# Full stacks in groups D, C and B, one bank pool in the MLP, and B's second wave on VectorE

## The chip, the cores and the metric

The kernel runs on one core of a Trainium2 chip. The metric is the device time of one launch in microseconds (us). The core has five engines that run their own instruction lists in order: TensorE (PE in the profile; its weight loads are PEld), VectorE (DVE), ScalarE (ACT), GpSimd (POOL) and SyncE (SP, which here only issues DMAs). Semaphores order the engines against each other.

## The reference

A trunk of two layers over a sequence of 1024 tokens and a width of 1024, in float32. Each layer normalises, projects once into the inputs of four groups of heads, and adds an output projection and a squared-ReLU MLP to the residual:

```python
for l in range(DEPTH):                       # DEPTH = 2, x is 1024 x 1024
    h = rms_norm(x, norm1_g[l])
    (a_cq, a_ckv, a_kr, b_q, b_k, b_v, c_q, c_k, c_v,
     d_q, d_k, d_v) = split(h @ w_in[l])
    y_a = mla_mixer(a_cq, a_ckv, a_kr, ...)   # latent attention, 4 heads
    y_b = diff_mixer(b_q, b_k, b_v, ...)      # 4 heads, two softmaxes each, 32 wide
    y_c = swa_mixer(c_q, c_k, c_v, ...)       # window of +-128, 4 q and 2 kv heads
    y_d = na_mixer(d_q, d_k, d_v, ...)        # neighbourhood on a 64-wide grid
    x = x + concat(norm(y_a), y_b, norm(y_c), norm(y_d)) @ w_out[l]
    h = rms_norm(x, norm2_g[l])
    x = x + square(relu(h @ w_up[l])) @ w_down[l]   # hidden width 4096
return rms_norm(x, final_norm_g)
```

In group B each of four heads has two pairs of a 32-wide q and k; its output is the first softmax less a factor times the second, times V. q and k are rotated first (rope).

## The kernel before

**Numbers in two parts.** Each float32 operand is split into a rounded high part and a low part, the rest (`split`, line 191): ScalarE rounds (L195), and VectorE or GpSimd subtracts (L189). A product of two such operands is three matmuls: high by high (L221), high by low (L222), low by high (L223). So one tile of output, 128 x 512, over a width of 1024 takes 8 x 3 = 24 matmuls. Weights come by DMA into `ws` (two buffers), are rounded into `wh` and split into `wl` by GpSimd (`weights`; `wtile` makes the two halves of a weight tile that 48 matmuls use, 24 for each half of the tokens). Each `load` is a request of SyncE.

**The opening of a layer.** In the first wave (`several`) six banks gather Q, K and V of B's first part (t = 0). Each is then evicted: `ev_rope` for Q and K (VectorE multiplies with the tables and writes a temporary `part`, three buffers; a second `part` holds the swapped halves, and an addition gives the rotated sum), then `emit_parts` splits it into `both`, high and low, whose DMAs store it in DRAM as `qb`, `kb`. V is put on the token axis by transposes (`to_values`) and stored as `vb`. Two of the three eviction steps of `ev_rope` and the splits go to the engine that `self.eng` names. The second wave projects Q, K and V of the second part (t = 1) into banks `mm`, `sb`, `mm`, with `self.eng` set to GpSimd. Then `weave` interleaves B's attention with the projections of groups A and D, which serve as filler. The PSUM banks of this part are mm=2, tr=2, sb=3, pv=1.

**Stacks.** q and k come back from DRAM as a stack (`self.stack()`): 128 partitions whose rows are high and low parts one under the other, so that one matmul of the scores (L851) sums the products of the parts. In B a stack of q holds high, high, low and that of k high, low, high, 32 rows each, 96 rows, by three loads each. D and C fill 128 rows with halves of 64, by two loads a stack.

**Order in this part.** A scheduler places every instruction by a simulated timeline and by priorities (`high_priority`), so the order on an engine is not that of the code.

**The MLP.** TensorE's order is written out by hand there. Up and down projections each run as seven block products in place of eight, over sums and differences of blocks. The up half works through groups with banks q=4, u=2, p=2; block products p1 to p7 go to them, and the results, squared and rectified, are stored to DRAM as `acts`, operands 1 to 7 of the down half among them. The last group ends with p7 (bank `u`), a copy of it to `u3` (L1290), p4 (bank `u`) and p3 (bank `p`). The down half opens another pool, u=4 and p=4, and loops over j = 0 to 3; in each j it multiplies the weight blocks `a11`, `a12`, `a21`, `a22` and their sums (four each, `raw` tiles by DMA, high and low as `wh` and `wl`) with operands loaded from `acts` (`act`, rounded into `far`). A block is 12 matmuls: four slices of its weights times three passes. The operands come in the order 1, 2, 6, 7, 4, 5, 3. `settled` is the sum behind which some of this may be issued; `finish_up` holds the last work of the up half, called from within the down half.

## Time and profile before

| | |
|---|---|
| median of 3 runs | 2625.5 us (2624.66 to 2625.53) |
| the profiled execution | 2624.3 us, its span 2622.5 us |
| granted TensorE clock, mean | 0.983 |
| DMA | 385 MB, 147 GB/s over the span |
| PE, share of the chain that ended last | 67% |

The profiled execution is the device time of one launch; its span runs from its first to its last instruction. In the rows of a timeline stand the start in us, the duration in us, the engine, the line, the operation, output and inputs, the shape, and in brackets how long the engine had been idle before and what released it. Rows whose first column is a stretch such as `70.00:80.00` are windows: the length, then busy time (and number of instructions) of PE, PEld, DVE, ACT, POOL, then the mean granted clock, the mean busy share of the DMA engines, and GB/s.

### The profile page before, as it was taken

What the parts mean: (1) busy time and instruction counts of PE and PEld (TensorE: products, weight loads), DVE (VectorE), ACT (ScalarE), POOL (GpSimd) and SP (SyncE); (2) the same over time, 40 slices, a digit from 0 to 9 for tenths busy, and PEclk for the clock granted to TensorE, in tenths of its full rate; (3) what the DMA queues carried; (4) which work ended last, traced back from release to release, by engine and by line L of the source; (5) the groups of instructions that cost most, each with busy time, mean ns of one, the idle gap of its engine ahead of it and who ended that gap; (6) DMA issues with size and microseconds to landing.
All of it is one profiled execution on the core that took longest, in us unless ns stands there. A gap on an engine that the chain in (4) does not pass through costs nothing.

```text
span 2622.5 us, 37463 instructions
## 1 busy us (share of the span) xinstructions
PE 2512.9 (96%) x12320; PEld 2087.0 (80%) x12320; DVE 1922.8 (73%) x3403; ACT 1427.7 (54%) x2588; POOL 1120.9 (43%) x800
## 2 busy tenths in 40 slices
PE   8999988999999999999999999899999999999998
PEld 7778877787788887888887888777887888878887
DVE  7577768784986668887576767677849866678886
ACT  4577767673644444444426777676736444444445
POOL 2565643201045554554434656332011555545554
PEclk9999999999999999999999899999999999999999
DMA  5634498332154456444245445962221544655431
GB/s 171 196 102 130 132 276 262 91 89 61 53 169 157 153 186 232 158 149 141 96 126 161 110 132 153 314 196 84 73 73 48 189 145 158 236 194 166 130 116 65
DMA packets 191539, 385.00 MB, mean 147 GB/s; under 512 B 23712, under 2 KB 34928, under 8 KB 191344
## 3 DMA queue, kind: packets, MB, share of 16 engines
q1 hardware_dynamic: 176976, 356.90, 44.1%
q10 hardware_dynamic: 14368, 25.70, 2.8%
q8 instruction: 98, 1.61, 0.3%
q14 instruction: 97, 0.79, 0.1%
HBM read 261.20 MB, written 121.32 MB: 146 GB/s over the span
## 4 chain that ended last, share of the span: by engine, by line
PE 67%; DVE 8%; issue 5%; ACT 4%; DMA 3%; POOL 1%; SPq 0%; DVEq 0%; POOLq 0%; ACTq 0%
PE u L223 9%; PE u L221 9%; PE u L222 9%; PE p L223 5%; PE p L222 5%; PE p L221 5%; PE mm L221 4%; PE mm L222 4%; PE mm L223 4%; PE sb L851 2%; DVE p L853 2%; PE tr L887 2%; ACT p L856 2%; DVE ptl L189 1%; DVE part L189 1%
## 5 line engine op out<-in xcount | busy, mean ns | idle before, releaser
L189 POOL TENSOR_TENSOR wl<-raw,wh 128x512 fp32r<-128x512 f32 x424 | 603.8, 1426 | 695.0 <-ACT wh L195 679.1
L195 ACT ACTIVATE wh<-raw 128x512 fp32r<-128x512 f32 x448 | 281.0, 629 | 545.9 <-PE u L222 297.8
L189 POOL TENSOR_TENSOR wl<-ws,wh 128x512 fp32r<-128x512 f32 (+1 forms) x120 | 150.1, 1253 | 413.1 <-ACT wh L195 386.5
L223 PE MATMUL u<-far,wl 128*128 128x512 f32 x768 | 301.5, 393 | 6.5 <-POOL wl L189 6.5
L221 PE MATMUL u<-far,wh 128*128 128x512 f32 x768 | 301.1, 392 | 4.9 <-ACT wh L195 2.7
L222 PE MATMUL u<-far,wh 128*128 128x512 f32 x768 | 300.8, 392 | 0.0
L189 DVE TENSOR_TENSOR ptl<-tr,pth 128x512 fp32r<-128x512 f32 (+2 forms) x384 | 237.5, 628 | 74.8 <-ACT pth L195 73.6
L189 DVE TENSOR_TENSOR raw<-raw 128x512 f32<-128x512 f32 x256 | 229.2, 904 | 84.7 <-DMA raw<-in_w_up 42.7
L856 ACT ACTIVATE p<-p,nm 128x1024 f32<-128x1024 f32 x192 | 220.2, 1147 | 83.3 <-DVE nm L853 82.5
L195 ACT ACTIVATE pth<-tr 128x512 fp32r<-128x512 f32 (+2 forms) x384 | 206.1, 547 | 94.4 <-PE tr L887 61.0
L223 PE MATMUL p<-far,wl 128*128 128x512 f32 (+1 forms) x648 | 251.0, 387 | 3.0 <-DVE wl L189 3.0
L221 PE MATMUL p<-far,wh 128*128 128x512 f32 (+1 forms) x648 | 250.9, 387 | 0.0
L222 PE MATMUL p<-far,wh 128*128 128x512 f32 (+1 forms) x648 | 250.6, 387 | 0.0
L851 PE MATMUL sb<-stack 96*128 96x512 f32 x640 | 218.6, 422 | 14.2 <-DVE part L189 8.9
L189 DVE TENSOR_TENSOR far<-act,far 128x512 fp32r<-128x512 f32 x224 | 199.4, 925 | 13.2 <-ACT far L195 13.2
L189 POOL TENSOR_TENSOR p<-p 128x1024 f32<-128x1024 f32 x64 | 154.0, 2409 | 109.2 <-ACT p L939 107.5
L221 PE MATMUL mm<-xh,wh 128*128 128x512 f32 x480 | 191.0, 398 | 4.6 <-DVE part L189 4.6
L223 PE MATMUL mm<-xh,wl 128*128 128x512 f32 x480 | 190.1, 396 | 0.0
L222 PE MATMUL mm<-xl,wh 128*128 128x512 f32 x480 | 189.2, 394 | 0.0
L223 PEld LDWEIGHTS u<-far,wl 128*128 128x128 f32 x768 | 145.3, 189 | 38.1 <-POOL wl L189 7.9
L221 PEld LDWEIGHTS u<-far,wh 128*128 128x128 f32 x768 | 145.4, 189 | 36.7 <-ACT wh L195 3.6
L222 PEld LDWEIGHTS u<-far,wh 128*128 128x128 f32 x768 | 145.2, 189 | 31.3 <-DVE far L189 0.8
(256 smaller groups left out, 5958.5 us busy)
## 6 DMA issues: line engine op xcount, KB each, us to landing
act<-acts SPq DMA_DIRECT2D x224, 256.0 KB
raw<-in_w_up SPq DMA_DIRECT2D x128, 256.0 KB
acts<-ev SPq DMA_DIRECT2D x128, 256.0 KB
raw<-in_w_down SPq DMA_DIRECT2D x128, 256.0 KB
acts<-ev ACTq DMA_DIRECT2D x96, 256.0 KB
ws<-in_w_in SPq DMA_DIRECT2D x76, 256.0 KB
rz<-drows SPq DMA_DIRECT2D x40, 256.0 KB
stack<-kd SPq DMA_DIRECT2D x32, 256.0 KB
```

The lines of the kernel that those rows point to most:

```text
L189: return (eng or self.nc.vector).tensor_tensor(out=out, in0=a, in1=b, op=op)
L195: self.rounded = nc.scalar.activation(hi, src, AF.Copy)
L221: mm(ps, w[0], x[0][:, sl], start=start, stop=False)
L222: mm(ps, w[0], x[1][:, sl], start=False, stop=False)
L223: mm(ps, w[1], x[0][:, sl], start=False, stop=stop)
L851: self.nc.tensor.matmul(ps, q[:, qt * P:(qt + 1) * P], k[:, sl], start=i == 0, stop=i == len(passes) - 1)
L853: self.nc.vector.tensor_tensor_reduce(out=p[:, sl], in0=ps, in1=self.zero[:, 0:1].bitcast(F).broadcast_to([P, 512]), scale=-scale, scalar= ...
L856: self.nc.scalar.activation(p, p, AF.Exp, bias=nm[:, 1:2], scale=-1.0, accum_out=z)
L887: nc.tensor.transpose(t[:, k * 256 + i * P:k * 256 + (i + 1) * P], p[:, (j * 2 + k) * P:(j * 2 + k + 1) * P], self.ident)
```

## The change

1. **Stacks.** `qb` is laid out in DRAM with the two parts of each row next to each other, so a stack of B's q is one load of 128 rows (high and low alternating); a stack of k is two loads, the high parts into the even and the low parts into the odd positions, each row twice (`twice`). The scores then run over 128 rows, with all four products of the parts where they had three. A stack of D or C is one load. On SyncE's queue a run has 1237 requests where it had 1333; those for B's stacks go from 96 to 48 a run.
2. **First wave.** V's two banks are now both `tr`, K's `sb` and `pv`, and V is evicted ahead of Q and K. V's transposes of the second part use `tr` too.
3. **Second wave.** `self.eng` is VectorE there. The weights of K and V (four `ws` loads a layer) are asked for by ScalarE. The call of `catch_up` between product and eviction is left out. Over the run, GpSimd has 16 instructions fewer and VectorE 16 more.
4. **MLP.** One pool of banks, q=4, u=2, p=2, spans both halves. The down half's four accumulators `u[]` take `q` banks, its other blocks alternate between `u` and `p`. p4 and p3 of the last group are called after the first down block (m = 0); the third sum is made ahead of them and `settled` is set there. The split of operand 1 is not bound to `settled`. Operand 4 is loaded from within the loop over operand 7, behind `summed` and the last rounding.

```diff
+def twice(t):
+    return t.unsqueeze(1).broadcast_to([t.shape[0], 2, *t.shape[1:]])
...
-        self.load(st, src)
+        (queue or self.nc.sync).dma_start(st, src)
...
-        qb, kb, vb = dr([2, 2, 4, 16, 2, S], "qb"), dr([2, 2, 4, 16, 2, S], "kb"), dr([4, P, 8, P], "vb")
+        qb, kb, vb = dr([2, 4, 16, 2, 2, S], "qb").rearrange("t g f h a s -> a t g f h s"), dr([2, 2, 4, 16, 2, S], "kb"), dr([4, P, 8, P], "vb")
...
-                    self.ev_plain(rb, self.to_values(vb[2 * t:2 * t + 2], "tr" if t else "mm"))]
+                    self.ev_plain(rb, self.to_values(vb[2 * t:2 * t + 2], "tr"))]
...
-                        return [(self.bank(a), self.bank(b)) for a, b in (("sb", "sb"), ("sb", "tr"), ("tr", "pv"))]
+                        return [(self.bank(a), self.bank(b)) for a, b in (("sb", "sb"), ("sb", "pv"), ("tr", "tr"))]
...
-                    for ev, b in zip(evacs_b(0), banks):
+                    q, k, v = zip(evacs_b(0), banks)
+                    for ev, b in (v, q, k):
                         for n in range(2):
                             ev(n, b[n])
-                    self.eng = nc.gpsimd
-                    for t, ev, tag in zip(self.WAVES[1], evacs_b(1), ("mm", "sb", "mm")):
-                        ws = self.wtile(w_in(t))
+                    self.eng = nc.vector
+                    for i, (t, ev, tag) in enumerate(zip(self.WAVES[1], evacs_b(1), ("mm", "sb", "mm"))):
+                        ws = self.wtile(w_in(t), nc.scalar if i else None)
                         for n in range(2):
                             ps = self.bank(tag)
                             self.product(ps, ws, xs, n)
-                            self.catch_up()
                             ev(n, ps)
+                    self.eng = nc.gpsimd
...
-                for i, (a, b) in enumerate(((0, 0), (0, 1), (1, 0))):
-                    self.load(qf[i * 32:(i + 1) * 32], run(qb[a, t, g]))
-                    self.load(kf[i * 32:(i + 1) * 32], run(kb[b, t, g]))
-                qk.append([(q[0:96], k[0:96])])
+                self.load(qf, twice(qb[:, t, g].rearrange("a f h s -> (f h a) s")))
+                for i in range(2):
+                    self.load(kf[i::2], twice(run(kb[i, t, g])))
+                qk.append([(q, k)])
...
-            self.mlp_up(l, acts)
-            self.mlp_down(l, acts)
+            with self.banks(q=4, u=2, p=2):
+                self.mlp_up(l, acts)
+                self.mlp_down(l, acts)
...
+            def third(s):
+                s.sum = self.tt(s.u3, s.p, s.u3, ALU.add)
...
-            p4(s)
-            p3(s)
+            third(s)
             self.settled = s.sum
+            def products():
+                p4(s)
+                p3(s)
...
-            self.finish_up = [free, rest]
+            self.finish_up = [products, free, rest]
...
-                u = [self.bank("u") for _ in M]
+                u = [self.bank("q") for _ in M]
...
+                b = [self.rows_split(self.far(), v) for v in t]
                 with ExitStack() as behind:
                     if j == 0:
                         behind.enter_context(tc.issue_after(self.settled.ins))
-                    b = [self.rows_split(self.far(), v) for v in t]
                     for m in M:
                         self.block(u[m], a11[m], b)
+                        if m == 0 and j == 0:
+                            self.finish_up.pop(0)()
...
-                        ps = self.bank("p")
+                        ps = self.bank("up"[m % 2])
...
-                with behind(passed):
-                    b = op(4)
+                    if m == 1:
+                        with behind(summed), behind(self.rounded):
+                            c = op(4)
+                b = c
...
-                p = [self.bank("p") for _ in M]
+                p = [self.bank("up"[m % 2]) for m in M]
```

What the order of the instructions becomes at three places follows. In a row stand the line, the operation, output and inputs, and the shape; a name's number tells instances apart, and differs between the two kernels.

The first place is GpSimd's order in the opening of layer 0, during the second wave: `wl` are its weight splits (`ws_571` and `ws_577` hold the weights of K, 655 and 661 those of V, 809 those of the first projection behind B), `part` and `both` the additions and splits of the evictions (524 and 530, 560 and 566 of Q's two halves, 608 and 614 of K's first). Before:

```order
L189 TENSOR_TENSOR wl_574<-ws_571,wh_573 128x512
L189 TENSOR_TENSOR wl_580<-ws_577,wh_579 128x512
L189 TENSOR_TENSOR part_524<-part_524,part_525 128x512
L189 TENSOR_TENSOR both_530<-part_524,both_530 128x512
L189 TENSOR_TENSOR wl_658<-ws_655,wh_657 128x512
L189 TENSOR_TENSOR wl_664<-ws_661,wh_663 128x512
L189 TENSOR_TENSOR part_560<-part_560,part_561 128x512
L189 TENSOR_TENSOR both_566<-part_560,both_566 128x512
L189 TENSOR_TENSOR wl_812<-ws_809,wh_811 128x512
L189 TENSOR_TENSOR part_608<-part_608,part_609 128x512
L189 TENSOR_TENSOR both_614<-part_608,both_614 128x512
```

After, from the same split on:

```order
L194 TENSOR_TENSOR wl_574<-ws_571,wh_573 128x512
L194 TENSOR_TENSOR wl_580<-ws_577,wh_579 128x512
L194 TENSOR_TENSOR wl_658<-ws_655,wh_657 128x512
L194 TENSOR_TENSOR wl_664<-ws_661,wh_663 128x512
L194 TENSOR_TENSOR wl_806<-ws_803,wh_805 128x512
L194 TENSOR_TENSOR wl_812<-ws_809,wh_811 128x512
L194 TENSOR_TENSOR wl_985<-ws_982,wh_984 128x512
```

Weight splits now follow one another; the additions and splits of the evictions have left this engine.

The second place is ScalarE's order in the same opening: `wh` are roundings of weights, `both<-part` those of the evictions of Q and K, `both<-mm` or `both<-tr` those of V, and DMA rows its requests (before, `wh_471` and `wh_477` are Q's weights; `both_427` and `both_438` are Q, 449 and 460 K). Before:

```order
L195 ACTIVATE wh_471<-ws_469 128x512
L195 ACTIVATE wh_477<-ws_475 128x512
L195 ACTIVATE both_427<-part_421 128x512
L195 ACTIVATE wh_573<-ws_571 128x512
L195 ACTIVATE both_438<-part_432 128x512
L195 ACTIVATE both_449<-part_443 128x512
L195 ACTIVATE both_460<-part_454 128x512
L195 ACTIVATE wh_579<-ws_577 128x512
L681 ACTIVATE both_511<-mm_506 128x8x64
L195 ACTIVATE wh_657<-ws_655 128x512
```

After:

```order
L200 ACTIVATE wh_489<-ws_487 128x512
L200 ACTIVATE wh_495<-ws_493 128x512
L212 DMA ws_571<-in_w_in 128x512
L212 DMA ws_577<-in_w_in 128x512
L200 ACTIVATE wh_573<-ws_571 128x512
L212 DMA ws_655<-in_w_in 128x512
L687 ACTIVATE both_428<-tr_423 128x8x64
L687 ACTIVATE both_439<-tr_434 128x8x64
L200 ACTIVATE wh_579<-ws_577 128x512
L200 ACTIVATE both_449<-part_443 128x512
L212 DMA ws_661<-in_w_in 128x512
L200 ACTIVATE wh_657<-ws_655 128x512
```

The roundings of V have moved ahead, the weight requests stand among the roundings, and `wh_579` and `wh_657` stand before the roundings of Q's two halves (`both_449`, and `both_460` behind the rows shown). On TensorE, the first score of B had 96 products and four transposes of the second wave ahead of it in the order; it has 20 + 28 + 48 + 44 = 140 products, with V's eight transposes after the first 20. Stretches of B's scores and value products with no projection product among them, longer than 24 instructions, were one in each layer (99 instructions with 17 scores in layer 0, 90 with 16 in layer 1) and are three (24, 53 and 95 instructions with 3, 11 and 14 scores in layer 0; 24, 59 and 41 with 3, 11 and 8 in layer 1).

The third place is ScalarE's order at the seam between the MLP's halves in layer 0. Of the weight roundings `wh`, those of `raw_10107` to `raw_10113` are the four blocks `a11`, those of `raw_10234` and `raw_10238` the first two of `a21`; `far<-act` are the roundings of operand 5. Before:

```order
L195 ACTIVATE wh_10358<-raw_10107 128x512
L195 ACTIVATE wh_10375<-raw_10109 128x512
L195 ACTIVATE far_10614<-act_10606 128x512
L195 ACTIVATE far_10617<-act_10608 128x512
L195 ACTIVATE wh_10392<-raw_10111 128x512
L195 ACTIVATE far_10620<-act_10610 128x512
L195 ACTIVATE wh_10409<-raw_10113 128x512
L195 ACTIVATE far_10623<-act_10612 128x512
L195 ACTIVATE wh_10446<-raw_10234 128x512
L195 ACTIVATE wh_10464<-raw_10238 128x512
```

After, where `raw_10027` to `raw_10033` are `a11`, `raw_10186` to `raw_10198` are `a21`:

```order
L200 ACTIVATE wh_10310<-raw_10027 128x512
L200 ACTIVATE wh_10327<-raw_10029 128x512
L200 ACTIVATE wh_10344<-raw_10031 128x512
L200 ACTIVATE wh_10361<-raw_10033 128x512
L200 ACTIVATE wh_10398<-raw_10186 128x512
L200 ACTIVATE wh_10416<-raw_10190 128x512
...
L200 ACTIVATE far_10658<-act_10650 128x512
L200 ACTIVATE far_10661<-act_10652 128x512
L200 ACTIVATE wh_10454<-raw_10194 128x512
L200 ACTIVATE wh_10472<-raw_10198 128x512
```

The four roundings of `a11` and two of `a21` stand together; behind them come ten activations (four of operand 4, four of operand 5 and the two shown of operand 3), then the other two of `a21`. TensorE's order at the seam was p7, p4, p3, then the down half's four blocks `a11`; it is p7, the block m = 0, p4, p3, the blocks m = 1 to 3, then the `a12` blocks alternating between banks `u` and `p`.

More of the change, by code (lines that the diff above doesn't have):

```diff
@@ L200, in split, with weights @@
                 out=lo, in0=src, scalar=scale, in1=hi.bitcast(F), op0=ALU.mult, op1=ALU.subtract)
-    def weights(self, src, pool=None, tag="w", bufs=3, keep=None):
+    def weights(self, src, pool=None, tag="w", bufs=3, keep=None, queue=None):
         pool = pool or self.wp
@@ L212, in weights, with wtile @@
         return [(wh[:, k], wl[:, k]) for k in range(n)]
-    def wtile(self, src):
-        return self.weights(src[0]) + self.weights(src[1])
+    def wtile(self, src, queue=None):
+        return self.weights(src[0], queue=queue) + self.weights(src[1], queue=queue)
     def passes(self, ps, w, x, sl, start, stop, **more):
@@ L1083, in attn_d @@
                 rows = slice(h2 * 64, (h2 + 1) * 64)
-                for i in range(2):
-                    half = slice(i * 64, (i + 1) * 64)
-                    self.load(qs.bitcast(F)[half], qd[i, t, rows])
-                    self.load(ks[0].bitcast(F)[half], kd[0, t, rows])
-                for i in range(2):
-                    self.load(ks[1].bitcast(F)[i * 64:(i + 1) * 64], kd[1, t, rows])
+                self.load(qs.bitcast(F), qd[:, t, rows].rearrange("i r s -> r i s"))
+                for i, k in enumerate(ks):
+                    self.load(k.bitcast(F), twice(kd[i, t, rows]))
                 v = self.vtile(vd[h])
@@ L1113, in attn_c @@
             for n, k in enumerate(ks):
-                for i in range(2):
-                    self.load(k.bitcast(F)[i * 64:(i + 1) * 64], run(kc[n, kv]))
+                self.load(k.bitcast(F), twice(run(kc[n, kv])))
             v = self.vtile(vc[kv])
@@ L1120, in attn_c @@
                 qs = self.stack()
-                for i in range(2):
-                    self.load(qs.bitcast(F)[i * 64:(i + 1) * 64], run(qc[i, kv, g]))
+                self.load(qs.bitcast(F), qc[:, kv, g].rearrange("a f h s -> (f h) a s"))
                 z, es, nm = (self.col(n, 8) for n in ("z0", "z1", "nb8"))
@@ L1228, in mlp_up @@
         sub = lambda o, a, b: self.tt(o, a, b, ALU.subtract)
-        with self.banks(q=4, u=2, p=2):
+        with ExitStack():
             near = lambda tag: [(self.piece(tag, R, "oph"), self.piece(tag, R, "opl")) for _ in range(4)]
@@ L1290, in p7 @@
                 nc.scalar.activation(s.u3, s.u, AF.Copy)
+            def third(s):
+                s.sum = self.tt(s.u3, s.p, s.u3, ALU.add)
             def p4(s):
-                s.sum = self.tt(s.u3, s.p, s.u3, ALU.add)
+                if s.sum is None:
+                    third(s)
                 self.block(s.u, s.c["22"], ops[4], start=False)
@@ L1320, in group @@
             def group(q):
-                s = SimpleNamespace(q=q, c=weights(q))
+                s = SimpleNamespace(q=q, c=weights(q), sum=None)
                 return s
@@ L1432, in mlp_up @@
                 held = s
-            p4(s)
-            p3(s)
+            third(s)
             self.settled = s.sum
+            def products():
+                p4(s)
+                p3(s)
             def free():
@@ L1458, in mlp_down @@
         sub = lambda o, a, b: self.tt(o, a, b, ALU.subtract)
-        with self.banks(u=4, p=4):
+        with ExitStack():
             def add(m, n, ps):
@@ L1516, in mlp_down @@
                     self.block(u[m], a11[m], b, start=False)
-                    add(m, 1, u[m])
+                    summed = add(m, 1, u[m])
                 with behind(passed):
@@ L1602, in final @@
             yield
-        ps = self.bank("u", [P, w // P])
+        ps = self.bank("q", [P, w // P])
         self.col_sums(ps, acc, self.ones[:, 0:1], range(w // P))
@@ L1609, in final @@
         yield
-        rb = self.bank("u")[:, :w]
+        rb = self.bank("q")[:, :w]
         for t in range(w // P):
```

## The prediction

> **What bounds the kernel now.** I read the page's head and chain first, then the timeline of TensorE with its idle times, and for each idle time the timelines of the engines behind it.
>
> ```profile
> span 2622.5 us, 37463 instructions
> PE 2512.9 (96%) x12320; PEld 2087.0 (80%) x12320; DVE 1922.8 (73%) x3403; ACT 1427.7 (54%) x2588; POOL 1120.9 (43%) x800
> PE 67%; DVE 8%; issue 5%; ACT 4%; DMA 3%; POOL 1%; SPq 0%; DVEq 0%; POOLq 0%; ACTq 0%
> ```
>
> TensorE is busy for 96% of the span and holds two thirds of the chain. The change alters none of its products in number or width, so the time can only move by TensorE's waits, and by matmuls that run at half pace after a wait. The undisturbed pace is 23.00/102 = 0.226 us for a 512-column matmul; the next stretch below it runs at half the granted clock, 13 matmuls in 5.60 us.
>
> ```profile
> 1037.00:1060.00 23.00, 23.00 (x102) 19.00 (x101) 13.21 (x17) 9.68 (x16) 10.77 (x9) 1.00 0.64 211
> 1031.40:1037.00 5.60, 5.60 (x13) 4.42 (x14) 4.96 (x7) 3.04 (x5) 3.47 (x3) 0.50 0.87 301
> ```
>
> I price a wait by start times: from the last matmul before it to the first at the old pace, less the nominal time of what ran between.
>
> **The opening of the attention: what it costs.** These are TensorE's rows around its waits, first layer 0, then layer 1.
>
> ```profile
> 57.23 0.39 PE L223 MATMUL sb<-xh,wl 128*128 128x512 f32 x1
> 58.95 0.66 PE L677 MATMUL mm<-ident,part 128*128 128x128 f32 x4 [1.34 <-DVE part L189]
> 60.39 0.39 PE L222 MATMUL sb<-xl,wh 128*128 128x512 f32 x1
> 61.29 0.50 PE L223 MATMUL sb<-xh,wl 128*128 128x512 f32 x1 [0.52 <-POOL wl L189]
> 83.53 0.39 PE L851 MATMUL sb<-stack 96*128 96x512 f32 x1
> 87.76 0.50 PE L851 MATMUL sb<-stack 96*128 96x512 f32 x1 [3.84 <-DVE part L189]
> 91.69 0.39 PE L222 MATMUL mm<-xl,wh 128*128 128x512 f32 x1
> ...
> 1355.41 0.39 PE L223 MATMUL sb<-xh,wl 128*128 128x512 f32 x1
> 1357.14 0.66 PE L677 MATMUL mm<-ident,part 128*128 128x128 f32 x4 [1.34 <-DVE part L189]
> 1358.58 0.40 PE L222 MATMUL sb<-xl,wh 128*128 128x512 f32 x1
> 1359.48 0.51 PE L223 MATMUL sb<-xh,wl 128*128 128x512 f32 x1 [0.50 <-POOL wl L189]
> 1381.73 0.39 PE L851 MATMUL sb<-stack 96*128 96x512 f32 x1
> 1387.15 1.53 PE L851 MATMUL sb<-stack 96*128 96x512 f32 x2 [5.03 <-DVE part L189]
> 1392.28 0.40 PE L222 MATMUL mm<-xl,wh 128*128 128x512 f32 x1
> ```
>
> The transposes of V cost 1.72 - 0.23 = 1.49 and 1.50 us, the late `wl` 0.67 and 0.67. The first scores cost more: between 83.53 and 91.69 stand three scores, four transposes and four products, nominally some 2.0 us, so 6.2 us are lost; in layer 1, 10.55 us less 2.65 (three more products) is 7.9. Together **18.4 us**: 4.3 small, 14.1 at the first scores. Who held the first scores is read one engine back at a time:
>
> ```profile
> 86.31 1.39 DVE L189 TENSOR_TENSOR part<-sb,tabs 64x512 f32<-64x512 f32 x2 [5.72 <-POOL part L189]
> 83.80 1.26 POOL L189 TENSOR_TENSOR wl<-ws,wh 128x512 fp32r<-128x512 f32 x1 [6.37 <-ACT wh L195]
> 85.02 1.26 POOL L189 TENSOR_TENSOR part<-part 128x512 f32<-128x512 f32 x1
> 83.09 0.63 ACT L195 ACTIVATE wh<-ws 128x512 fp32r<-128x512 f32 x1 [7.03 <-DMA ws<-in_w_in]
> 79.23 0.36 SPq L160 DMA_DIRECT2D ws<-in_w_in  x1
> ```
>
> The score needs its `sb` bank, which VectorE empties for B's K of the second wave. VectorE waits for GpSimd's add, because that add frees a `part` buffer. GpSimd is in order and its add stands behind a weight split that waits for weights, which SyncE asked for only among the stack loads.
>
> **What the change does there.** GpSimd's eight second-wave operations per layer go to VectorE, so its order holds weight splits alone and no `part` buffer hangs on a weight transfer. V of the first wave is evicted first; its transposes now stand behind 20 products (4.5 us) instead of waiting. In the new order the first score stands behind 20+28+48+44 = 140 products and eight transposes of the second wave, where it was behind 96 and four; this gives the stacks time. Added work: 16 VectorE operations in all, against a row like the second below some 0.65 us each, 10.4 us, laid where VectorE stood idle for up to 5.72 us. If that cover failed, the bank of the second wave's V would be late.
>
> Is anything late next? The second wave starts at 46.58.
>
> ```profile
> 46.58 0.39 PE L221 MATMUL mm<-xh,wh 128*128 128x512 f32 x1
> 44.08 1.39 DVE L189 TENSOR_TENSOR part<-sb,tabs 64x512 f32<-64x512 f32 x2
> 49.25 0.69 DVE L189 TENSOR_TENSOR both<-part,both 128x512 fp32r<-128x512 f32 x1
> 1360.64 5.33 DMA kb<-both
> ```
>
> So TensorE reaches the first score at about 46.58 + 140 x 0.226 + 0.7 = 79 us. ScalarE's order now has the weight requests and splits between the roundings (`both<-part`), and the split before Q's second rounding waits for a weight buffer that Q's products free at about 46.58 + 48 x 0.226 + 0.7 = 58 us. From there VectorE needs some 2.7 us for each remaining half (0.69 + 1.39 + 0.6), with the last K half stored at about 66 to 67; a store took 5.33 us to land in layer 1, so the stacks are asked for at 72 and, with about 4 us to load, stand at 76 to 77, 2 to 3 us ahead of TensorE. I take the whole 18.4 us as gained, with this thin cover.
>
> The stacks themselves: 96 DMA issues fewer at about 0.4 us each come off SyncE's queue, which is on 0% of the chain, so I count nothing; some waits elsewhere that end on a load may shrink, by up to 3 us. B's scores use 128 rows instead of 96; products of 128 and scores of 96 rows take the same 0.39 us above, so nothing. B's loads grow from 768 to 1024 KB a pair, 1 MB for the four pairs of a part, and here the DMA engines are full:
>
> ```profile
> 70.00:80.00 10.00, 10.00 (x46) 8.26 (x45) 5.60 (x10) 0.63 (x1) 4.36 (x4) 1.00 0.99 286
> ```
>
> At 286 GB/s 1 MB is 3.7 us, half of it before the first two pairs; the bounds are 0 (behind other products) and 3.7 us a layer, and I take 0, the row's share of 0.99 being kept for a rival. The Trainium skill, DMA: Bandwidth & Descriptors, section Issuing engines are not separate DMA queues, says that requests from ScalarE and SyncE run on the same 16 engines, so that moving them saves issue time alone. By that rule, if the 7.03 us were transfer time, the 14.1 us at the first scores would stay. The row's share of 0.99 agrees with full engines; how much of the 7.03 us was transfer no row tells.
>
> **The seam between the MLP's halves.**
>
> ```profile
> 990.11 0.50 PE L221 MATMUL u<-far,wh 128*128 128x512 f32 x1 [1.09 <-ACT ev L1290]
> 2288.58 0.50 PE L221 MATMUL u<-far,wh 128*128 128x512 f32 x1 [1.09 <-ACT ev L1290]
> 1025.00:1038.00 13.00, 8.30 (x24) 5.97 (x23) 12.36 (x17) 5.75 (x10) 8.14 (x4) 0.74 0.90 302
> 2324.00:2337.00 13.00, 8.50 (x27) 6.17 (x27) 11.83 (x17) 5.80 (x11) 8.64 (x4) 0.74 0.84 297
> 1017.83 2.04 SPq L160 DMA_DIRECT2D raw<-in_w_down  x2
> 1023.59 0.93 SPq L160 DMA_DIRECT2D act<-acts  x2
> 1026.17 0.63 ACT L195 ACTIVATE far<-act 128x512 fp32r<-128x512 f32 x1 [7.06 <-DMA act<-acts]
> 1027.39 6.85 POOL L189 TENSOR_TENSOR wl<-raw,wh 128x512 fp32r<-128x512 f32 x3 [6.18 <-ACT wh L195]
> ```
>
> The wait of 1.09 us is the copy of bank `u` between two blocks of the last group; start to start it costs about 1.25. With one bank pool a block of the down half goes between these two, 12 x 0.226 = 2.7 us of cover, so twice 1.25 = 2.5 go. The large one: 24 matmuls took 13 us instead of 5.43, 7.6 lost, and 27 instead of 6.10 in layer 1, 6.9 lost. Its cause is ScalarE's order: the weight rounding of the fourth `a11` block stands behind the third activation of operand 5, whose load SyncE held behind next weights until 1023.59; then GpSimd needed 6.85 us for three splits. In the new order the four `a11` roundings and two of `a21` stand together and these activations come after. So 2.5 + 7.6 + 6.9 = **17.0 us** go.
>
> What is late next: the third `a21` rounding stands behind ten activations, some 0.55 us each. Blocks last 2.7 us and a rounding can start when the block three earlier ends; on that count ScalarE begins the ten 8.8 us after the first `a11` block starts and ends them at 14.4, then rounding and split need 0.6 + 1.3 to 2.3, against a need at about 16.7: 0 to 0.6 us late if the loads are in time. I take 0.35 a layer, **0.7** back. If a load is late, the old price of about 7 us returns.
>
> **A cost in the middle of B.** Without projection products between them, the scores of B wait for the softmax:
>
> ```profile
> 145.00:170.00 25.00, 20.87 (x95) 15.85 (x95) 19.99 (x54) 19.45 (x33) 22.35 (x16) 0.80 0.40 117
> 1447.00:1469.00 22.00, 20.80 (x82) 15.47 (x81) 17.01 (x50) 16.63 (x28) 18.84 (x16) 0.69 0.37 112
> ```
>
> Idle and clock together lose 4.1 + 0.20 x 20.87 = 8.3 us here and 1.2 + 0.31 x 20.80 = 7.6 in layer 1. The order of before has one such stretch of 17 and 16 scores; the new order has three, with 3 + 11 + 14 and 3 + 11 + 8 scores (those over 24 instructions long). Bounds: all gone (-15.9) and twice the price (+15.9). By scores, leaving out the short first ones, it is 8.3 x 25/17 - 8.3 = 3.9 and 7.6 x 19/16 - 7.6 = 1.4; counting the three in layer 1 too, 2.9. I take 3.9 + 2.9 = **6.8 us** back.
>
> **The sum.** 18.4 + 17.0 - 0.7 - 6.8 = 27.9 us. The profiled execution took 2624.3 us, its span and 1.8 around; that is 1.2 below the median of 2625.5. 2624.3 - 27.9 + 1.2 = **2598 us**.
>
> **Rivals.**
> - *The stacks are late* (0.20). DMA share 0.99 and a cover of 2 to 3 us speak for it; the 44 further products ahead of the first score against. The 14.1 us stay: 2612.
> - *The seam's wait moves* (0.10) to the third `a21` block, behind the ten activations; against it, their loads are issued some 10 us before. 14.5 - 0.7 return: 2612.
> - *B's stretches shrink* (0.13), since the softmax starts sooner: instead of 6.8 back, half of the 15.9 gained: 2583.
> - *It does not do what it says* (0.08): both large waits only change place, and 4.3 + 2.5 are eaten by B's 6.8: 2625.
> - *Slower: ScalarE's queue holds the roundings* (0.06). A weight request that waits for GpSimd, or a split that waits for a buffer, stops every rounding behind it, VectorE's subtraction after it, and the bank that V needs. The order shows two roundings held for half a weight tile's 24 products, 5.4 us; V's bank is then free about 3 us ahead. If four were held for 5.4 us each, 21.6 less 3 a layer, 37 in all, would turn the gain into 2635. It decides from 33/2 + 3 = 20 us a layer on.
>
> **Chances.** Forecast 0.43. About 0.2% is what a measurement of this kernel can tell from no change, 5 us. Faster: 0.43 + 0.20 + 0.10 + 0.13 = 0.86; same 0.08; slower 0.06. The range takes in the first four cases with 4 to 5 us at each end for the rest of the order, which is recast everywhere: 2578 to 2616.
>
> **What would show it.** Right: no wait of TensorE over 1 us before the first scores; none at about 25 us behind the seam and none on `ev` at its start; a rest of under 1 us at the third `a21` block. Wrong: a wait of scores on a `stack` load; half clock in the first 60 us of the second wave; B's stretches costing over 20 us a layer; a SyncE queue whose stack loads wait longer than before.

## The result, and the profile after

The changed kernel takes 2608.6 us (median of 5 runs, 2605.45 to 2612.07) where the kernel before took 2624.7 (median of 5): a ratio of 0.9943, 95% interval 0.9932 to 0.9954. That is 16 us gained; forecast were 27.9. The profiled execution took 2608.62 us, its span 2606.8. The head of its page:

```profile
span 2606.8 us, 37344 instructions
PE 2503.4 (96%) x12320; PEld 2082.2 (80%) x12320; DVE 1952.0 (75%) x3419; ACT 1426.0 (55%) x2588; POOL 1099.5 (42%) x784
PE 74%; DVE 10%; ACT 5%; issue 4%; DMA 4%; POOL 2%; SPq 0%; DVEq 0%; ACTq 0%; POOLq 0%
```

VectorE has gained 29 us of work and GpSimd lost 21; TensorE's instructions are as many as before. (VectorE's 16 operations more are about 10 of it, at the prediction's 0.65 us each; 15 are the group `far<-act`, whose mean rose from 925 to 993 ns.) Now the two places of the prediction. From the timeline, TensorE's rows at the first scores, layer 0 and layer 1, and SyncE's requests in front of those of layer 0:

```profile
78.83 0.70 PE L857 MATMUL sb<-stack 128*128 128x512 f32 x2
...
84.90 0.47 PE L857 MATMUL sb<-stack 128*128 128x512 f32 x1 [1.70 <-issue]
...
1373.43 0.70 PE L857 MATMUL sb<-stack 128*128 128x512 f32 x2 [1.08 <-issue]
...
72.28 1.24 SPq L172 DMA_DIRECT2D qb<-both  x2
74.02 1.45 SPq L165 DMA_DIRECT2D stack<-kb  x2
75.52 0.60 SPq L165 DMA_DIRECT2D stack<-qb  x1
76.16 1.26 SPq L172 DMA_DIRECT2D qb<-both  x2
77.46 2.91 SPq L165 DMA_DIRECT2D stack<-kb  x2
```

The waits of 3.84 and 5.03 us are gone, and those on V's transposes and on the weights too. In their place stand 1.70 and 1.08 us that no engine is named for. In layer 0 it is a k stack's load (e10, in the same order, names it), that of the second pair, asked for from 77.46 on behind the stores of Q's second wave. In layer 1 the wait at the same place has no name in e10 either (0.80 us there), so that it is a load, too, is likely and not shown. At the seam, windows of 13 us from the `a11` blocks on and windows around the third and fourth `a21` block, layer 0 and layer 1:

```profile
1025.00:1038.00 13.00, 13.00 (x59) 10.78 (x58) 10.67 (x14) 8.82 (x17) 7.65 (x5) 1.00 0.83 267
1040.00:1048.00 8.00, 7.01 (x30) 5.22 (x29) 8.00 (x11) 2.78 (x6) 2.77 (x2) 1.00 0.83 264
2311.00:2324.00 13.00, 13.00 (x59) 10.76 (x58) 10.68 (x14) 8.82 (x17) 7.62 (x5) 1.00 0.85 268
2326.00:2334.00 8.00, 7.00 (x30) 5.24 (x29) 8.00 (x11) 2.79 (x6) 2.78 (x2) 1.00 0.81 262
```

The two rows of TensorE's timeline with a wait in the second of these windows:

```profile
1041.23 0.47 PE L226 MATMUL q<-far,wh 128*128 128x512 f32 x1 [0.46 <-DVE x L194]
...
1044.74 0.47 PE L226 MATMUL q<-far,wh 128*128 128x512 f32 x1 [0.54 <-ACT wh L200]
```

13 us now hold 59 matmuls (24 before) at full clock. What is left is about 1 us of idle time at the third and fourth `a21` blocks.

**Stage by stage.** To compare executions I took TensorE's instructions of each trace in order, counted each at its pace (0.226 us per 512 columns, 64 columns at least; 2272.9 us in all), and read off the start times at which 80, 250, 480, 840, 920, 1150, 1225, 1400, 1600, 1960 and 2050 us of it had been issued: they close the opening, B, the rest of the attention (D, C, A), the MLP up to the seam, and the seam, in both layers. Below is each stage's time less that of the profiled execution before. The order of the instructions on TensorE within the attention of layer 0 is the same for kernels with the same letter; in layer 1 the changed kernel, e7, e8 and e10 agree, and e5 with e9.

| kernel | order | opening 0 / 1 | B 0 / 1 | D, C, A 0 / 1 | seam 0 / 1 | rest | span |
|---|---|---|---|---|---|---|---|
| changed | a | -7.4 / -8.5 | +3.8 / +2.6 | +6.3 / +1.0 | -6.6 / -6.7 | -0.1 | -15.7 |
| e7 the same | a | -8.3 / -7.8 | +2.1 / +1.4 | -0.3 / +4.9 | -6.6 / -6.6 | +0.6 | -20.7 |
| e8 operand 5 | a | -8.1 / -8.6 | +1.7 / +2.9 | +3.8 / +5.1 | -8.1 / -8.1 | +0.1 | -19.3 |
| e2 attention | a | -8.0 / -8.8 | +4.1 / +3.7 | +7.8 / +1.6 | -1.5 / -2.6 | +0.5 | -3.3 |
| e10 V first | a | -8.0 / -7.9 | +4.0 / +3.7 | +3.8 / +3.0 | -8.1 / -8.2 | +1.0 | -16.6 |
| e1 MLP | before | +1.1 / -1.1 | +0.1 / +4.8 | +3.4 / +7.5 | -6.6 / -6.5 | +0.6 | +3.4 |
| e3 stacks | s | -4.4 / -4.4 | +1.7 / -0.4 | -1.4 / +3.3 | -4.6 / +0.1 | -1.3 | -11.3 |
| e5 stacks, MLP | s | -3.2 / -6.3 | -0.5 / +0.6 | -1.6 / -1.7 | -6.6 / -6.6 | +1.2 | -24.8 |
| e9 e5, operand 5 | s | -4.3 / -6.3 | -0.1 / +2.0 | +1.0 / +2.1 | -8.1 / -8.2 | +0.4 | -21.5 |
| e4 waves | w | -7.9 / -8.5 | +1.8 / +3.4 | +12.2 / +5.3 | -2.3 / -1.1 | +1.8 | +4.7 |
| e6 waves, MLP | w | -3.7 / -8.5 | -0.7 / +5.4 | +10.1 / +3.0 | -6.6 / -7.3 | +1.3 | -7.0 |
| e11 B's stacks | other | -2.7 / -6.6 | -0.6 / -0.2 | +11.2 / +9.6 | -4.9 / -3.9 | +1.7 | +3.6 |
| e12 VectorE | other | +2.5 / +2.2 | -0.4 / +2.1 | +7.1 / +15.2 | -1.5 / -0.9 | +2.8 | +29.3 |

So in the changed kernel the openings give 15.9 us and the seams 13.3; B takes 6.4 back, D, C and A another 7.3. The rows also show how far one trace can be trusted: the seam repeats to 0.1 us, D, C and A of layer 0 in one and the same order differ by 8 us (-0.3 to +7.8). Only medians size that stage.

**B's stretches.** Windows over the two longer of the three stretches that the prediction named, layer 0 and layer 1:

```profile
134.00:153.00 19.00, 12.51 (x69) 8.98 (x68) 14.04 (x39) 14.99 (x26) 16.32 (x15) 0.88 0.72 249
183.00:203.00 20.00, 17.77 (x98) 12.32 (x96) 18.25 (x54) 17.98 (x31) 10.48 (x7) 1.00 0.53 184
1427.00:1449.00 22.00, 15.14 (x69) 12.35 (x69) 15.35 (x43) 15.59 (x28) 18.75 (x16) 0.77 0.63 212
1484.00:1493.00 9.00, 8.02 (x46) 5.93 (x45) 7.52 (x22) 8.54 (x15) 6.11 (x4) 1.00 0.69 182
```

Idle and clock together lose 8.0 and 2.2 us in layer 0, 10.3 and 1.0 in layer 1: 21.5 us, where by the prediction the one stretch in each layer of before lost 15.9 together.

### The profile page after: what moved, and what is told of

Its sections match the earlier page's. It is cut to its first block, busy times and chain, and to the rows that moved or that the text cites. A ratio compares the mean times of both kernels' runs of the same rounds, so it can differ in the third digit from the quotient of the medians.

```text
span 2606.8 us, 37344 instructions
## 1 busy us (share of the span) xinstructions
PE 2503.4 (96%) x12320; PEld 2082.2 (80%) x12320; DVE 1952.0 (75%) x3419; ACT 1426.0 (55%) x2588; POOL 1099.5 (42%) x784
## 4 chain that ended last, share of the span: by engine, by line
PE 74%; DVE 10%; ACT 5%; issue 4%; DMA 4%; POOL 2%; SPq 0%; DVEq 0%; ACTq 0%; POOLq 0%
PE u L226 6%; PE u L227 6%; PE u L228 6%; PE mm L226 6%; PE mm L227 5%; PE mm L228 5%; PE q L226 5%; PE q L227 5%; PE q L228 5%; PE p L228 4%; PE p L227 4%; PE p L226 4%; DVE p L859 3%; PE sb L857 2%; PE tr L893 2%
## 5 line engine op out<-in xcount | busy, mean ns | idle before, releaser
L857 PE MATMUL sb<-stack 96*128 96x512 f32 (+1 forms) x640 | 213.5, 413 | 11.4 <-DVE nm L859 8.1
L194 DVE TENSOR_TENSOR far<-act,far 128x512 fp32r<-128x512 f32 x224 | 214.4, 993 | 10.8 <-ACT far L200 10.8
L226 PE MATMUL q<-far,wh 128*128 128x512 f32 x512 | 199.5, 390 | 2.0 <-ACT wh L200 1.1
L227 PE MATMUL q<-far,wh 128*128 128x512 f32 x512 | 199.4, 389 | 0.7 <-DVE far L194 0.7
L228 PE MATMUL q<-far,wl 128*128 128x512 f32 x512 | 199.2, 389 | 0.0
L228 PE MATMUL p<-far,wl 128*128 128x512 f32 (+1 forms) x452 | 175.6, 389 | 3.0 <-DVE wl L194 3.0
L226 PE MATMUL p<-far,wh 128*128 128x512 f32 (+1 forms) x452 | 175.5, 388 | 0.0
L227 PE MATMUL u<-far,wh 128*128 128x512 f32 (+1 forms) x452 | 175.2, 388 | 0.0
L227 PE MATMUL p<-far,wh 128*128 128x512 f32 (+1 forms) x452 | 175.2, 388 | 0.0
L226 PE MATMUL u<-far,wh 128*128 128x512 f32 (+1 forms) x452 | 175.0, 387 | 0.0
L228 PE MATMUL u<-far,wl 128*128 128x512 f32 (+1 forms) x452 | 175.0, 387 | 0.0
```

The source lines that it names most:

```text
L194: return (eng or self.nc.vector).tensor_tensor(out=out, in0=a, in1=b, op=op)
L226: mm(ps, w[0], x[0][:, sl], start=start, stop=False)
L227: mm(ps, w[0], x[1][:, sl], start=False, stop=False)
L228: mm(ps, w[1], x[0][:, sl], start=False, stop=stop)
L857: self.nc.tensor.matmul(ps, q[:, qt * P:(qt + 1) * P], k[:, sl], start=i == 0, stop=i == len(passes) - 1)
```

## The experiments

Ratios are to runs of the kernel before on the same chip in the same session. The median there was 2624.4 for e1 to e4, 2623.7 for e5 to e8 and 2624.3 for e9 to e12.

### The parts alone: e1 to e4

e1 takes part 4 of the change alone, e2 parts 1 to 3, e3 part 1, e4 parts 2 and 3. Their diffs are those pieces of the change; the cores are

```diff
# e1
+            with self.banks(q=4, u=2, p=2):
+            self.finish_up = [products, free, rest]
# e3 (and e2)
+                self.load(qf, twice(qb[:, t, g].rearrange("a f h s -> (f h a) s")))
+                self.load(qs.bitcast(F), qd[:, t, rows].rearrange("i r s -> r i s"))
# e4 (and e2)
+                    for ev, b in (v, q, k):
+                    self.eng = nc.vector
+                        ws = self.wtile(w_in(t), nc.scalar if i else None)
```

> The kernel before with the MLP's part of the change alone (one bank pool, p4 and p3 behind the first down block, operand 4 from within the loop). Theory (the parts add): the seam keeps what the trace of the changed kernel shows, 0.9 + 8.0 - 1.5 us in layer 0 and 0.7 + 7.1 - 1.2 in layer 1, 14.0 in all, less 1.2 at the very end of the program, so some 12.8 below the kernel before, ratio 0.995, and the attention's 2 x 14 us of waits stay as they were. Rival (the seam's gain hangs on the earlier finish of the attention, or on queues that the fewer stack loads empty): less than 9 us. Rival for the end: if the 1.2 us at the end are a matter of the attention's change they are absent here and it is 14.0.

Measured: 2623.3 us, ratio 0.9996 (0.9985 to 1.0007). The seams gave 6.6 and 6.5 us in its trace, nearly the 14 expected, but the whole gave about 1. So the theory that the parts add fell; the rival's number (under 9) holds, but not its reason, since the seam's gain is there. Layer 1's attention, whose order changed with this part though no line of it did, cost 11.2 us more in this execution (-1.1 + 4.8 + 7.5). Layer 0, where the order is that of before, cost 4.6 more in this execution; that is the spread of one trace, since the profiled execution took 2627.7, 4.4 above its median.

> The kernel before with the stacks and the two waves of the change, the MLP as before. Theory (the gain of the opening is given back within the attention): the opening gains 7 us in layer 0 and 8.5 in layer 1, B's stretches return 5 and 2.5, the rest of the attention of layer 0 some 4 to 5: 2 to 4 us below the kernel before, ratio 0.9985 to 0.999. Rival (the opening's gain is kept and the two traces only differ by chance further on): 12 to 15 us below, ratio 0.995.

Measured: 2619.9 us, ratio 0.9980 (0.9968 to 0.9992): 4.5 gained, just above the 2 to 4 of the theory. The opening's 16.8 us are given back in B, D, C and A (17.2 in this trace).

> The kernel before with the stacks of D, C and B alone. Theory (the first scores hang on GpSimd's order, where an addition stands behind a weight split): the wait before the first scores stays at 4 to 6 us in both layers, the small waits of 1.3 and 0.5 stay, and the time is within 4 us of before. Rival (the weights were late because SyncE was busy with 96 stack requests): the wait falls by more than half and 6 to 10 us are gained.

Measured: 2614.5 us, ratio 0.9962 (0.9947 to 0.9976). The rival had the size: 9.9 us gained, the openings 4.4 us shorter each. How, is shown by timeline rows of e5, whose TensorE order in layer 0 is the same: TensorE's first long wait, two rows of GpSimd, two of SyncE. The last row is from the kernel before.

```profile
85.26 0.66 PE L682 MATMUL tr<-ident,part 128*128 128x128 f32 x4 [2.13 <-DVE part L194]
...
76.45 1.31 POOL L194 TENSOR_TENSOR part<-part 128x512 f32<-128x512 f32 x1
81.96 1.29 POOL L194 TENSOR_TENSOR wl<-ws,wh 128x512 fp32r<-128x512 f32 x1 [4.20 <-ACT wh L200]
...
73.20 0.74 SPq L165 DMA_DIRECT2D ws<-in_w_in  x1
76.00 0.89 SPq L165 DMA_DIRECT2D ws<-in_w_in  x1
...
77.05 0.37 SPq L160 DMA_DIRECT2D ws<-in_w_in  x1
```

The scheduler put GpSimd's addition (76.45) in front of the split instead of behind it, and with fewer requests ahead the weights were asked for earlier. There are two `ws` buffers, and each request follows the split two before it; counted so, the split at 81.96 uses the weights asked for at 73.20, and the late split of the kernel before those asked for at 77.05. (The row of 79.23 in the prediction's chain is the request for the other half of that tile.) The request went out 3.9 us earlier, but ScalarE's rounding of these weights began only 1.8 us earlier (81.25, not 83.09), and 0.9 of that is a lead that the whole trace had before (TensorE's first transposes at 58.02, not 58.95). So the earlier request can have given about 1 us here, by estimate from these rows; the rest most likely comes with the addition's new place. The two were not tried apart.

> The kernel before with V evicted first, the second wave evicted by VectorE and its weights asked for by ScalarE; stacks of 96 rows with their many loads as before. Theory (this part removes the opening's waits, the stacks' loads decide how late the first scores are): V's and the weights' waits go (4.3 us in both layers), the first scores wait for stacks some 2 to 5 us in place of 1.7 and 1.1 us in the changed kernel, and B gives back about as much as in the changed kernel: 0 to 5 us gained. Rival (the single-load stacks do nothing for the first scores): waits of 1 to 2 us as in the changed kernel.

Measured: 2628.4 us, ratio 1.0012 (1.0000 to 1.0024): no gain, 4 us lost. The openings gained 7.9 and 8.5 us, more than with the stacks alone, and the waits at the first scores are 0.87 and 0.86 us, on loads of `kb`, where the changed kernel has 1.70 and 1.08. So the theory's 2 to 5 us fell, and the rival was right in that the new stacks do nothing for the first scores here. D, C and A cost 12.2 and 5.3 more. In C of layer 0 the longest stretch without a projection product had 99 instructions before and has 141 in this order. The window over that stretch in the kernel before:

```profile
424.00:443.00 19.00, 16.76 (x100) 14.12 (x99) 14.34 (x39) 14.37 (x40) 6.51 (x8) 0.92 0.93 297
```

The same stretch in e4, and in e6, which has e4's order there:

```profile
419.00:448.00 29.00, 24.01 (x143) 18.87 (x142) 23.00 (x65) 22.89 (x65) 7.54 (x9) 1.00 0.88 236
418.00:450.00 32.00, 27.14 (x143) 23.02 (x142) 21.95 (x62) 22.32 (x64) 6.68 (x9) 0.84 0.74 204
```

TensorE is idle for 2.2 us of 19 before, for 5.0 of 29 in e4 and for 4.9 of 32 in e6, there at a lower clock. Its waits in these windows end on VectorE, behind the scores and values. That is a few of the 12.2 us; where the rest lies was not traced.

### The pairs, and the change once more: e5 to e8

e5 is parts 1 and 4, e6 parts 2 to 4, e7 the changed kernel. e8 is the changed kernel with

```diff
-                b = c
+                b, turned = c, self.rounded
...
-                b = op(5)
+                with behind(turned):
+                    b = op(5)
```

> The change without its second part: stacks and MLP, the waves as before. In layer 0 the attention's order is that of the kernel with the stacks alone. Theory A (the seam's gain is kept everywhere, and what decides besides it is the order that the scheduler gives each layer's attention): some 14 us at the seam less 1.2 at the end, and the 4 us or so of layer 0 that the stacks alone showed; layer 1 has a new order, worth +-6: 2607, between 2601 and 2613. Theory B (the MLP's part is worth the 1 us that its run alone measured, and the parts add): 2613 to 2614.

Measured: 2599.6 us, ratio 0.9905 (0.9889 to 0.9921). Theory A, at the good end, and the fastest kernel of the study.

> The change without the stacks. Theory A: the seam's 14 us less 1.2 at the end, and the 6 us that layer 0 lost with the waves alone come back as a loss: 2618, between 2612 and 2624 for the new order of layer 1. Theory B (parts add): 2627. If 2608 is reached, the stacks matter for nothing.

Measured: 2619.9 us, ratio 0.9983 (0.9974 to 0.9993), as theory A had it.

> The changed kernel once more, on the chip of the other runs, for a second trace of the same program. Theory A (executions of one program differ by some us in the attention of groups B, D, C and A, where TensorE waits for many short chains): the MLP's and the seam's times repeat within 0.3 us, the attention's of a layer differ from the first trace by up to 4 us. Rival (the differences between the traces are all due to the order): both layers' attention repeats within 1 us. The median is 2608 to 2612 either way.

Measured: 2606.4 us, ratio 0.9939 (0.9923 to 0.9955), the same as the first time, though 1.6 below the 2608 to 2612 expected. The seams repeat to 0.1 us; the D, C and A of layer 0 differ by 6.6 us, more than the 4 expected.

> The changed kernel with the roundings of operand 5 (and with them those of operand 3) bound behind the rounding of the last a21 block in the first j, so that four activations and not ten stand before the third a21 rounding; the order on TensorE within both layers' attention is the same as in the changed kernel. Theory (the rest of the seam's wait at the third a21 block is ScalarE's order): its 0.54 us wait goes in both layers and the seam gains 0.7 us each, 1.4 in all, below what the times can tell. Rival (the bank or the load is what holds it): the wait stays within 0.2 us of 0.54, or a later block takes it over with 1 us or more.

Measured: 2605.4 us, ratio 0.9934 (0.9922 to 0.9946). The seams are 8.1 us below before, 1.5 a layer better than in the changed kernel, where 0.7 was expected. The window around the third and fourth `a21` blocks has no idle time left:

```profile
1041.00:1048.00 7.00, 7.00 (x32) 5.82 (x31) 7.00 (x12) 4.22 (x7) 3.40 (x3) 1.00 0.90 273
```

So the rest of the seam's wait was the ten activations on ScalarE, as the prediction had named it, at four times its price.

### Inside the waves: e9 to e12

e9 is e5 with e8's edit. e10 adds to e9 only the order and the banks of the first wave; e11 is the kernel before with B's stacks alone; e12 is the kernel before with `self.eng` left at VectorE in the second wave, and nothing else:

```diff
# e10, on e9
-                    for ev, b in zip(evacs_b(0), banks):
+                    q, k, v = zip(evacs_b(0), banks)
+                    for ev, b in (v, q, k):
# e12, on the kernel before
-                    self.eng = nc.gpsimd
                     for t, ev, tag in zip(self.WAVES[1], evacs_b(1), ("mm", "sb", "mm")):
...
+                    self.eng = nc.gpsimd
```

> Stacks and MLP as in e5, with operand 5 bound behind the last a21 rounding as in e8; TensorE's order within both attentions is that of e5. Theory (the waves are a net cost, the seam's rest is ScalarE's order): e5's 2599.6 less 1.5 to 3, so 2597 to 2598 and the fastest of all; the seams 8.1 below before. Rival (e5 was favoured by chance in layer 1): 2603 or more, with layer 1's attention 4 us or more above e5's.

Measured: 2601.1 us, ratio 0.9914 (0.9901 to 0.9927): the same as e5 within the intervals, between the theory's 2597 to 2598 and the rival's 2603. The seams are 8.1 and 8.2 below before; the further 3 us are too small to show in the times.

> e9 with V of the first wave evicted first, with the change's banks; the second wave is evicted by GpSimd and VectorE as before and all weights are asked for by SyncE. TensorE's order within both attentions becomes, row for row, that of the changed kernel. Theory A (what the waves cost in B, D, C and A comes from TensorE's order): the attention behind the opening costs what it does in e7 and e8, the opening some 2 us a layer more for GpSimd's chain, so 2605 to 2610. Rival B (the cost is VectorE's added work and ScalarE's requests): the attention behind the opening returns to e9's and the time lies within 3 us of e9.

Measured: 2608.0 us, ratio 0.9939 (0.9925 to 0.9952): theory A. Without VectorE's added work and without ScalarE's requests the openings gain 8.0 and 7.9 us, against 8.1 and 8.6 with both (e8), and the time is the changed kernel's. V first and its banks are what acts, most likely through TensorE's order, which is the changed kernel's row for row. They cost 7 us against e9: by the table 5.8 in B and 3.7 in D, C and A, with 5.3 won at the openings. What is left in front of the scores is the load, as TensorE's row of e10 says:

```profile
84.31 0.50 PE L857 MATMUL sb<-stack 128*128 128x512 f32 x1 [1.55 <-DMA stack<-kb]
```

The Trainium skill, DMA: Bandwidth & Descriptors, section Issuing engines are not separate DMA queues, says that requests run on the same 16 DMA engines whichever engine starts them, and that starting them on several saves sequencer time alone. The openings with ScalarE's requests and VectorE's added work (e8, 16.7 us) and without both (15.9 us) differ by 0.8 us, which fits.

> The kernel before with B's stacks alone; D's and C's loads as before. Theory (the gain of the stacks is B's, since the requests in front of the weights at the opening are B's): the opening gains 4.4 us in both layers as with all stacks, and the time is 2613 to 2618. Rival (the loads of D and C count, in the region of D and C): half of it or less, 2619 or more.

Measured: 2628.6 us, ratio 1.0020 (1.0010 to 1.0029). Against the theory, and on the rival's side (2619 or more): the openings gain 2.7 and 6.6 us, but D, C and A cost 11.2 and 9.6 more, where with D's and C's stacks (e3) they cost -1.4 and +3.3. TensorE's waits there end on VectorE's and ScalarE's chains, not on loads of stacks, so the other order is the likelier cause; the loads of D and C and the order were not tried apart.

> The kernel before with the second wave evicted by VectorE alone; order of the first wave, banks, queues and stacks as before. Theory (the wait at the first scores is GpSimd's addition behind a weight split): V's 1.5 and the weights' 0.7 stay in both layers, the wait on VectorE's part at the first scores goes, and in its place stands a wait on stacks of 0 to 2 us, so the opening gains 3 to 6 us a layer. Rival (bandwidth holds the first scores): a wait on a stack's load of 3 us or more takes its place and the opening gains less than 2.

Measured: 2653.3 us, ratio 1.0114 (1.0100 to 1.0129): both theories fell, it is slower by 29 us. Of these the table puts 4.7 at the openings and 22.3 in D, C and A, where TensorE's order is another one; why that part costs so much was not traced. From the timeline of e12, TensorE's wait at the first score, and behind it VectorE, ScalarE and SyncE:

```profile
87.40 0.51 PE L851 MATMUL sb<-stack 96*128 96x512 f32 x1 [3.67 <-DVE part L189]
...
83.33 1.41 DVE L189 TENSOR_TENSOR both<-part,both 128x512 fp32r<-128x512 f32 x1 [5.97 <-ACT both L195]
...
82.14 0.63 ACT L195 ACTIVATE wh<-ws 128x512 fp32r<-128x512 f32 x1 [12.55 <-DMA ws<-in_w_in]
82.68 0.62 ACT L195 ACTIVATE both<-part 128x512 fp32r<-128x512 f32 x1
...
76.57 0.37 SPq L160 DMA_DIRECT2D ws<-in_w_in  x1
```

The wait of before is 3.84 us and here 3.67 (in layer 1 5.03 and 4.91). GpSimd is out of the eviction, but the rounding of the late weights stands on ScalarE in front of the eviction's rounding, idle for 12.55 us, and VectorE's subtraction waits behind that. Each engine takes its list in order, so the late weight holds the eviction wherever the two share one.

## Why the prediction was right, and where not

The time lies in the range and on the side forecast, 10.6 us above the predicted value. Two of the signs that the prediction named for being wrong are there: waits of over 1 us before the first scores, and in layer 0 on a `stack` load. That the time lies in the range all the same is owed to the range's width: a cost that is not in the sum took 7.3 us. Of the 12.2 us by which the trace's gain (15.7) falls short of the sum (27.9), the terms take these shares.

- **The opening, 18.4 forecast, 15.9 measured.** The waits named are gone, and the cover of "2 to 3 us" for the stacks was too thin by 1.7 and 1.1 us: the k stacks were asked for at 74 to 80 us, not at 72, since SyncE's order has stores of the second wave in front of them, and in layer 0 the second pair's scores started 6.1 us after the last of their k requests (78.78), where the prediction had "about 4 us to load" without a row. That is the first rival, at a small price.
- **Its reason was wrong.** The step that failed is "GpSimd's eight second-wave operations per layer go to VectorE, so its order holds weight splits alone and no `part` buffer hangs on a weight transfer". I had read the chain of waits down to SyncE's late request (to the wrong one of two rows, 79.23 for 77.05), and then credited the removal of one link in the middle. e12 does just that and keeps the wait, because the `part` buffer then hangs on the late weight by way of ScalarE; e10 leaves that link in place and has openings as short as with it removed. What goes with a shorter wait is GpSimd's addition in front of the split (the stacks, e3 and e5, with about 1 us for the earlier request) or 44 more products ahead of the first score (V first, e10); the stacks and the waves together gain no more at the openings than the waves alone, 15.9 against e4's 16.4. So the gain came by V first, which the prediction had down as time for the stacks, and not by the step that it credited. In that it was lucky.
- **The stacks at "nothing".** Alone they are worth 9.9 us. In the trace 8.8 of it lie at the openings, and 4.6 at the seam of layer 0; that seam gives 1.5 to 4.9 us in e2, e4, e11 and e12 too, where the MLP is that of before; the reason is open. "SyncE's queue, which is on 0% of the chain" was no ground: the chain counts SyncE's own time, not the transfers that stand in its list, nor the order that the scheduler gives to the rest.
- **The seam, 16.3 forecast, 13.3 measured.** Cause and edit were right: e8's 16.2 is close to the 17.0 without give-back. The give-back at the third and fourth `a21` blocks was 2.9, not 0.7.
- **B, 6.8 back forecast, 6.4 measured**, 3.5 to 7.8 in the other traces of that order (e2's layer 1 has another). The stretches named hold most of it, 5.6 us by the windows above, but not evenly by scores as the sum had it: the stretches of 11 scores lose 8.0 and 10.3, those of 14 and 8 scores 2.2 and 1.0.
- **D, C and A, not in the sum, 7.3 back**, 4.6 to 9.4 in the others. I had allowed 4 to 5 us at each end of the range for "the rest of the order" and looked at no row of it. This stage and B decide which version wins: the order with V first is 6.8 us slower than the one without it (e7 2606.4, e5 2599.6), although its openings are shorter.
- **Slower by ScalarE's queue (0.06).** That rival's mechanism is seen in e12, a weight in front of a rounding, with another weight; there the openings lose 4.7 us. In the changed kernel no rounding of Q or K in the second wave of layer 0 stands behind a weight that is still on its way.

That parts add, the theory of e1, was wrong too: by the medians the MLP's part is worth 1 us on the kernel before, 8 on the waves, 14 on the stacks and 13 on both, with seams 13.1 to 13.9 us below before in all four traces. What differs is the order that the scheduler gives to attention that no line of the part touches, and the seams without the part, which are 2.4 to 8.8 us below before in e2 to e4, e11 and e12. Why one order costs D, C and A ten microseconds more than another is open, but for a few in the long stretch in C that e4 and e6 show. The best version found is e5, the change without the waves (2599.6), with e9 equal to it.

## What to carry to other kernels

When a chain of waits leads through three engines to a late request, make the request earlier, or put the work that others wait for in front of the instruction that waits for it; taking one engine out of the middle can let the wait pass through the next engine's list, as in e12. Under a scheduler every edit recasts the order of regions it does not touch: test each part alone and in pairs, and compare by stage, because a gain of 14 us can vanish in a region where executions of one program differ by 8. Where a later part of a change treats a wait that an earlier part already shortens, leave it out and measure.

## What the runs showed of the hardware

In two windows the DMA engines were equally busy and moved different amounts: the prediction's window of 70 to 80 us has a share of 0.99 at 286 GB/s before; in e5 the share is the same and the rate 351.

```profile
70.00:80.00 10.00, 10.00 (x45) 8.27 (x45) 7.57 (x13) 0.63 (x1) 5.14 (x4) 1.00 0.99 351
```

The DMA view of e5 has 16 loads of q stacks at 512 KB where that of before has 48 at 128 KB; the q loads also write 128 rows where they wrote 32. That the size or the rows of the loads make the rate is the likely reading; neither was tried alone, and the windows hold other transfers too.

```profile
stack<-qb SPq DMA_DIRECT2D x16, 512.0 KB
```

A second observation is at the very end of the program. The first of three small operations of VectorE, from the timeline of before (the other two took 0.16 us each; GpSimd was idle until 2613.12):

```profile
2612.47 0.15 DVE L267 SCALAR_TENSOR_TENSOR rs_t<-rs_r 128x2 f32<-128x2 f32 x1
```

The same three after, and what GpSimd did beside them:

```profile
2595.77 0.69 DVE L272 SCALAR_TENSOR_TENSOR rs_t<-rs_r 128x2 f32<-128x2 f32 x1
2596.50 0.65 DVE L194 TENSOR_TENSOR rs_t<-rs_t,ms 128x2 f32<-128x2 f32 x1
2597.18 0.65 DVE L274 SCALAR_TENSOR_TENSOR rs_r<-rs_t,rs_r 128x2 f32<-128x2 f32 x1
...
2595.72 2.08 POOL L194 TENSOR_TENSOR two<-x,ev 128x256 f32<-128x256 f32 x3 [3.61 <-ACT ev L1628]
```

Each took 0.65 to 0.69 us in place of 0.15 to 0.16, about as long as one of GpSimd's three multiplications (2.08/3 = 0.69): 1.5 us at a place where nothing hides it. The Trainium skill, SBUF — State Buffer, section SBUF: two separate sides, has VectorE and GpSimd share a pair of ports that, when VectorE's operation has two inputs in SBUF and GpSimd's reads SBUF, one of them holds for a whole instruction while the other blocks; these rows agree.
